# One denoising step of a hybrid trunk: the RWKV-7 stage divided along the tokens, and adaLN by single columns with stationary weights

## The chip, the cores and the metric

The kernel runs on one core of a Trainium2 chip. The metric is the device time of one execution, in microseconds (us). It was timed in several runs of the same program, and one further execution was profiled. The engines work side by side, each with its own queue, and wait for each other by semaphores: PE (TensorE, matrix products; PEld is its weight load), DVE (VectorE), ACT (ScalarE), POOL (GpSimd) and SP (SyncE, which here issues most transfers).

## The reference

One step of a two-layer network over a prompt of 256 tokens and a sample of 1024 tokens, 1024 channels. The even layer runs differential attention and a bidirectional RWKV-7 side by side; the odd layer mixes by Fourier transforms; each layer ends in a gated MLP. The change touches the RWKV and the modulation (adaLN). Cut to these:

```python
for l in range(DEPTH):                       # adaLN: 6144 columns of two conditions, for each layer
    mod = jax.nn.silu(c) @ w_ada[l] + b_ada[l]
...
def wkv_scan(state0, r, w, k, v, kk, a):     # 8 heads of 64, each direction by itself
    def step(S, inp):
        r_t, w_t, k_t, v_t, kk_t, a_t = inp
        sa = jnp.einsum("bhij,bhj->bhi", S, -kk_t)
        S = (S * w_t[:, :, None, :] + sa[..., None] * (kk_t * a_t)[:, :, None, :]
             + v_t[..., None] * k_t[:, :, None, :])
        return S, jnp.einsum("bhij,bhj->bhi", S, r_t)
...
for d in range(2):                           # forward and backward
    decay = jnp.exp(-jnp.exp(-jax.nn.softplus(-(w0 + jnp.tanh(wd) @ w2)) - 0.5))
    a = jax.nn.sigmoid(a0 + ad @ a2)
    kd = k * (1 + (a - 1) * kvec[1])
    S, y = wkv_scan(s0[:, d], r, decay, kd, v, kk, a)
    ys = ys + y
    bonus = bonus + jnp.sum(rh * kdh * r_k, axis=-1, keepdims=True) * vh
y = (layernorm_by_head(ys) * lnx[0] + lnx[1] + bonus) * (sigmoid(gd) @ g2)
```

## The kernel before

The heads are taken as 4 pairs (128 channels each). Time is cut into chunks of 64 tokens (C = 64). Inside a chunk the recurrence is a triangular system, so that a chunk's work is a handful of small matrix products, and only a 64 x 64 state for each head and direction goes from chunk to chunk. A *unit* is one direction of one pair over 256 tokens (4 chunks).

The stage has five *jobs*, one after the other: the sample of each pair (16 chunks, both directions, 8 units), and at last the prompt of all four pairs (8 units). The steps of a job, with the lines of the page:

- `job_prep`, 16 steps: `piece_prep` loads r, k, v of 256 tokens, sums squares by head (`hs_ps`, L737) and transposes v (`fl_ps`, L747). `unit_values` makes decays and the scaled k, r (`lora_ps` L753, scan L810, `bk` L838 to L844, `bkw` L847, `bd` L854). `unit_products` makes the products inside the chunks (`G_ps` L866), masks them (DVE, L870), gathers the diagonal 32 x 32 blocks (`il`, L873), sums the bonus and transposes `bkw`.
- `inverses`: a forward substitution of all 32 x 32 blocks of the job at once, on DVE alone: two transposes (L918, L919), 31 pairs of a product (L928) and a sum (L932), each on the result of the one before, two transposes back (L938, L939). Behind it stand the *corrections* of the units: T is copied into `tz` (ACT, L961), products mq (L965), ms (L969), gv (L975), tb (L983) and their copies on ACT (L987, L988).
- `chains`, 16 steps: at each, for both directions, state times keys (`ch`, L1035), `sav` from it (DVE, L1044), the state's increment (L1054), the new state (`sbd`, DVE, L1069, one instruction for each head), and the output (`y_ps`, L1080, L1082). The last output sum is DVE's L1092.
- `job_post`: y is normalised by head, gains and bonus are added, the gate is multiplied in (L1111 to L1143).

The modulation's columns that later stages need (20 blocks of 512 columns) are made beside this, by `ada_blocks`. A block loads weights in pieces of 256 KB (`ada_w`), multiplies them as the moving operand (128x512, L188) with the two conditions as stationary ones, copies the result (L195), and turns it into columns by four 128x2 products (L199).

All engines run in program order. `run` sets it: it takes steps of several generators in turns, in the proportion of the numbers beside them. So a job's chains (13 steps) stand beside 11 steps of the next job's preparation and 29 steps of adaLN; the last 3 chain steps stand beside the inverse, 5 steps of preparation beside the corrections. The preparation of job 0 is written ahead of all that, and the scheduler places it between the last tiles of the attention (`attn_tiles`, whose last instruction for each tile is `yt`, L568). Tiles with the same tag share buffers; G tiles have 6 slots for each direction.

Of the kernel before, what the change touches and what calls it, by code (L numbers as in the profile page):

```python
# [2 lines left out]

# [34 lines left out]
def host_tables():  # L38
# [36 lines left out]
    # columns: cos of channel frequencies 0 .. 64, sin of 1 .. 63 (and its negative)  # L75
# [23 lines left out]
def hybrid_step(ctx: ExitStack, tc: tile.TileContext, i: dict, o: dict):  # L99
# [16 lines left out]
    yab_d = tc.dram_tile([D, T], F32, name="yab_d")  # L116

    def reverse_rows(dst, src, a, n):
# [20 lines left out]
    def mm3(ps, a, b, first, last):  # L139
        """ps += a.T @ b for operands split into (hi, lo) float32r parts."""  # L140
# [5 lines left out]
    # modulation by channel [part, cond, block]; its gates (parts 2, 5) also by row, in mod_d  # L146
# [27 lines left out]
    def ada_steps(l, j, wp, pp, tag, nb, kn, wb, sb):  # L174
        """Columns 512 j of the modulation, in steps; its weights come by kn blocks."""
# [47 lines left out]

    def mod_cols(l, part):
        """[128, cond, KD] columns of one part of the modulation."""
# [4 lines left out]
    def hcols(pair, q, t0, n):  # L230
        """Tokens t0 .. t0 + n of part q (hi, lo) of one channel block; its tiles are (sample, prompt) by part."""
# [49 lines left out]
    def norm_scale(pl, tj, f, xs):  # L281
        """xs = f * rms(f) ** -1 of [128 tokens, D]; tj: (tag, bufs) of the squares."""
# [7 lines left out]
    def norm_tile(pl, tt, pp, tag, nb, xs, t0, hh, A, B):  # L290
        """Modulated, channel-major parts hh[k] = (hi, lo) of the 128 scaled tokens xs from t0."""
# [26 lines left out]
    def post_norm(xp, f, gg, res_ap, out_ap, rows=128, skip=0):  # L318
        """out = res + gate * rmsnorm(f); f [rows, D] in SBUF, overwritten."""
# [12 lines left out]
    # ================= layer 0: mixer input =================  # L332
    with ExitStack() as st:
# [44 lines left out]
        # values  # L378
# [33 lines left out]
        # queries, keys and RWKV projections, with the differential attention beside them  # L412
        with ExitStack() as st2:
# [35 lines left out]
            def do_fb(ti):  # L449
# [18 lines left out]
                if ti in (12, 14):  # L468
                    # wd: tanh; gd: sigmoid = 0.5 tanh(x / 2) + 0.5
# [16 lines left out]
            # -(exp(s0) - exp(s1) + lam_init)  # L486
# [27 lines left out]
                    # exp(s - max of the chunk) and its sum, by chunks of the keys  # L514
# [14 lines left out]
                    # factors exp(max of the chunk - max) / sum, times -lambda for the second map  # L529
# [107 lines left out]
    def out_weights(fw, wp, ks):  # L637
        """Rows of the even layer's output projection, split."""
# [9 lines left out]
    def out_product(fw, fo, po, t0):  # L648
        """The even layer's output projection of 128 tokens."""
# [15 lines left out]
    # ================= layer 0: RWKV-7 =================  # L665
    with ExitStack() as st:
        # by the times at which the memory becomes free and is needed again: lt from the chains on, eg from the
        # preparation on; ex (units that the last job does without), ep and li (preparation and inverses) are given
        # back before the last chains
# [5 lines left out]
        li = pool(st_d, "li", side="right")  # L675
        pp = pool(st, "pp2", space=PSUM)
        st_0 = ExitStack()
        PG = [pool(st_0, "p0", space=PSUM, side="right")]
# [14 lines left out]
        nc.vector.tensor_scalar(out=wa0, in0=wa0, scalar1=0.5, scalar2=None, op0=ALU.mult)  # L693
        kv1h = eg.tile([128, 2, 4], F32, name="kv1h")
        nc.vector.tensor_scalar(out=kv1h[:, 0, :], in0=kv[:, 1, :], scalar1=0.5, scalar2=None, op0=ALU.mult)
        nc.vector.tensor_scalar(
            out=kv1h[:, 1, :], in0=kv[:, 1, :], scalar1=-0.5, scalar2=1.0, op0=ALU.mult, op1=ALU.add
        )
        bonk = eg.tile([128, 4, 2], F32, name="bonk")
        for p in range(4):  # L700
            nc.vector.tensor_scalar(out=bonk[:, p, :], in0=bones, scalar1=kv[:, 2, p:p + 1], scalar2=None, op0=ALU.mult)
        cmask = eg.tile([128, 256], F32, name="cmask")
# [3 lines left out]
        sbd = [[lt.tile([128, 128], F32, name=f"sbd{d}{j}") for j in range(4)] for d in range(2)]  # L706
        for d in range(2):
            for j in range(4):
                nc.gpsimd.memset(sbd[d][j], 0.0)
        # b and k by head; T, by direction: the rest stays zero  # L710
        bds = [ep.tile([128, 4, 2, 128], F32, name=f"bd{j}") for j in range(2)]
        tzs = [[li.tile([128, 4, 2, 64], F32, name=f"tz{d}{j}") for j in range(2)] for d in range(2)]
        for t_ in bds + tzs[0] + tzs[1]:
            nc.gpsimd.memset(t_, 0.0)
        nw = [0, 0, [0, 0]]
        slot = [0, 0]
        LOB = 1
        NA = 13
        NB = 5
        A0, A1, A2, B1, B2, B3, B4 = 0, 16, 8, 29, 0, 0, 0  # L720
        NT, NCJ = 8, 16
        NP, NTP, NCP = 256, 2, 4
# [3 lines left out]
        jobs = [[(p, NP * j) for j in range(4)] for p in range(4)]  # L726
        jobs.append([(p, LS) for p in range(4)])

        c3 = lambda t: t.rearrange("p (c s) -> p c s", s=C)

        fl = lambda t: t.rearrange("p a b -> p (a b)")

        def head_sums(src, wt, out, acc):
            """out[tok, tile, head] (+)= sum over channels of src [channel, tok] wt [channel, head]."""
            ps = PG[0].tile([128, NTP, 2], F32, tag="g", bufs=2, name="hs_ps")
            for j in range(NTP):
                nc.tensor.matmul(ps[:, j, :], lhsT=src[:, j * 128:(j + 1) * 128], rhs=wt, start=True, stop=True)  # L737
            if acc is None:
                nc.vector.tensor_copy(out, ps)
            else:  # L740
                nc.vector.tensor_tensor(out=out, in0=ps, in1=acc, op=ALU.add)

        def flips(n, src):
            """Transposes of n 128 x 128 blocks src(j) into one bank."""
            ps = PG[0].tile([128, 4, 128], F32, tag="g", bufs=2, name="fl_ps")
# [4 lines left out]
        def lora(first, p, d, src, w, which, out):  # L750
            """out = tanh(0.5 (w0 + src @ w)) for the pair's channels."""
            ps = PG[-1].tile([128, NP], F32, tag="g" if first else "lo", bufs=2 if first else LOB, name="lora_ps")
            nc.tensor.matmul(ps, lhsT=w[HS[d], which, :], rhs=src[HS[d], which, :], start=True, stop=True)  # L753
            nc.scalar.activation(out, ps, AF.Tanh, bias=wa0[:, which, d, p:p + 1], scale=0.5)

        def piece_prep(J, j):
            p, t0 = J["pcs"][j]
            j0 = NTP * j
            if J.get("wp") != p:
                J["wp"] = p  # L760
                J["w"] = ep.tile([128, 2, 128], F32, tag="w2", bufs=2, name="w2")
                for e, nm in enumerate(("rwkv_w2", "rwkv_a2")):
                    for d in range(2):
                        nc.sync.dma_start(out=J["w"][HS[d], e, :], in_=i[nm][0, d, :, p * 128:(p + 1) * 128])
            r = ep.tile([128, NP], F32, tag="r", bufs=4, name="r")
            k = ep.tile([128, NP], F32, tag="k", bufs=4, name="k")
            v = ep.tile([128, NP], F32, tag="tmp", bufs=2, name="v")
            nc.sync.dma_start(out=k, in_=fb_d[4 + p, :, t0:t0 + NP])
            nc.sync.dma_start(out=v, in_=fb_d[8 + p, :, t0:t0 + NP])
            nc.sync.dma_start(out=r, in_=fb_d[p, :, t0:t0 + NP])  # L770
            # kk = k kv0 / sqrt(sum over the head + 1e-12); kkh = 0.5 kk
# [3 lines left out]
            head_sums(sq, bones, ss, None)  # L775
            nc.scalar.copy(J["vt"][:, j0:j0 + NTP, :], flips(NTP, lambda e: v[:, e * 128:(e + 1) * 128]))
# [6 lines left out]
            kkh = ep.tile([128, NP], F32, tag="kkh", bufs=4, name="kkh")  # L783
# [1114 lines left out]
```

## Time and profile before

| what | us |
|---|---|
| median of 3 runs | 3827.24 |
| lowest, highest run | 3824.96, 3835.42 |
| span of the profiled execution | 3829.1 |
| busy in the span: PE, DVE, ACT, POOL | 3568.9, 1984.3, 1381.8, 570.5 |
| first inverse's start, last output sum's start | 725.3, 1609.6 |
| chains, first to last `sav` (five jobs) | 852.8 to 1603.2 |
| corrections, first to last tb | 803.2 to 1560.7 |

The profile gives no other time for its execution than the span, which is 1.9 us above the median. A busy PE is not PE at its peak: the clock that was granted to it is a column of its own in the tables by window, and 0.50 there means that a product takes twice as long. A group's busy time is a sum over the instructions of one line, and can overlap itself, since products are pipelined; the distance from start to start is the better price where PE never waits.

### The profile page before, as it was taken

The numbers are of one execution on the slowest core, as the hardware profiler recorded it, in microseconds if no ns is written. First come the engines' busy times: TensorE is split into PE (matmuls) and PEld (weight loads), VectorE is DVE, ScalarE is ACT, GpSimd is POOL, SyncE is SP. The second block draws the span as 40 slices with busy tenths as digits, with TensorE's granted clock in tenths as the row PEclk, the third lists the DMA queues.
The fourth block names the chain that finished last, engine by engine and source line by source line (L and its number), as shares of the span: only waits on it lengthen the run. The fifth ranks groups of instructions, "written<-read, shape, count | busy, mean of one in ns | idle before, by whom it ended". The sixth has DMA issues, their size and how long they took to land.

```text
span 3829.1 us, 53177 instructions
## 1 busy us (share of the span) xinstructions
PE 3568.9 (93%) x20712; PEld 2865.0 (75%) x20712; DVE 1984.3 (52%) x4009; ACT 1381.8 (36%) x2892; POOL 570.5 (15%) x937
## 2 busy tenths in 40 slices
PE   6999999898999786999999999998968999999997
PEld 5888887554646575788888888887757888888886
DVE  4276677837372847565344434446554344443446
ACT  4266566652535353463212111113443211121211
POOL 3111112411212222053000000004141000000003
PEclk8999999879897967999999999999988999999999
DMA  6232323223342210455111111104341111111113
GB/s 215 92 97 81 98 67 86 83 76 118 97 119 75 67 29 7 125 151 140 39 33 45 39 34 39 39 31 172 126 115 32 39 39 34 44 34 39 39 31 129
DMA packets 293469, 286.60 MB, mean 75 GB/s; under 512 B 52955, under 2 KB 229051, under 8 KB 293217
## 3 DMA queue, kind: packets, MB, share of 16 engines
q1 hardware_dynamic: 228864, 223.09, 18.9%
q0 software_dynamic: 15952, 40.46, 3.1%
q10 hardware_dynamic: 48400, 19.65, 2.1%
q8 instruction: 163, 2.67, 0.3%
q14 instruction: 90, 0.73, 0.1%
HBM read 233.65 MB, written 51.51 MB: 74 GB/s over the span
## 4 chain that ended last, share of the span: by engine, by line
PE 79%; DVE 7%; DMA 4%; ACT 3%; issue 2%; POOL 1%; ACTq 0%; DVEq 0%; SPq 0%; POOLq 0%
PE a_ps L142 11%; PE a_ps L143 10%; PE a_ps L141 10%; PE b_ps L142 5%; PE b_ps L141 5%; PE b_ps L143 5%; PE ada_ps L188 3%; PE tb_ps L983 2%; PE f_ps L141 2%; PE f_ps L142 2%; PE f_ps L143 2%; PE sc_ps L520 2%; PE G_ps L866 2%; PE pv_ps L556 2%; DMA ada_w<-in_w_ada 1%
## 5 line engine op out<-in xcount | busy, mean ns | idle before, releaser
L141 PE MATMUL a_ps<-hh,f_hi 128*128 128x512 f32 (+1 forms) x2144 | 761.4, 356 | 18.7 <-ACT f_hi L136 14.5
L142 PE MATMUL a_ps<-hl,f_hi 128*128 128x512 f32 (+1 forms) x2144 | 762.5, 356 | 3.1 <-POOL hl L308 3.1
L143 PE MATMUL a_ps<-hh,f_lo 128*128 128x512 f32 (+1 forms) x2144 | 761.1, 355 | 0.2 <-DVE f_lo L137 0.2
L1313 DVE TENSOR_TENSOR acc<-b_ps,acc 128x512 f32<-128x512 f32 x400 | 270.4, 689 | 405.7 <-PE b_ps L143 405.6
L141 PEld LDWEIGHTS a_ps<-hh,f_hi 128*128 128x128 f32 x2144 | 404.6, 189 | 83.6 <-ACT f_hi L136 15.0
L142 PEld LDWEIGHTS a_ps<-hl,f_hi 128*128 128x128 f32 x2144 | 404.7, 189 | 68.3 <-POOL hl L308 4.8
L143 PEld LDWEIGHTS a_ps<-hh,f_lo 128*128 128x128 f32 x2144 | 405.0, 189 | 63.0 <-DVE f_lo L137 0.9
L142 PE MATMUL b_ps<-d_lo,mh 128*128 128x512 f32 x880 | 348.4, 396 | 0.0
L143 PE MATMUL b_ps<-d_hi,ml 128*128 128x512 f32 x880 | 346.8, 394 | 0.0
L141 PE MATMUL b_ps<-d_hi,mh 128*128 128x512 f32 x880 | 341.5, 396 | 3.6 <-DVE acc L1313 3.1
L137 DVE TENSOR_TENSOR f_lo<-f_raw,f_hi 128x512 fp32r<-128x512 f32 x176 | 114.5, 691 | 307.2 <-ACT f_hi L136 305.0
L1259 POOL MEMSET gp<- 128x1 f32 x44 | 4.3, 98 | 1572.7 <-DVE cv L1278 1572.7
L136 ACT CAST d_hi<-d_raw 128x512 fp32r<-128x512 f32 x88 | 54.5, 621 | 488.4 <-PE b_ps L143 474.6
L141 PE MATMUL f_ps<-hh,w_hi 128*128 128x512 f32 (+1 forms) x552 | 198.5, 360 | 0.5 <-ACT nk L444 0.5
L141 PEld LDWEIGHTS b_ps<-d_hi,mh 128*128 128x128 f32 x880 | 165.3, 188 | 45.0 <-DVE acc L1313 4.5
L188 PE MATMUL ada_ps<-ada_w,csil 128*32 128x512 f32 x384 | 172.6, 721 | 28.0 <-DMA ada_w<-in_w_ada 26.4
L142 PE MATMUL f_ps<-hl,w_hi 128*128 128x512 f32 (+1 forms) x552 | 197.3, 357 | 0.0
L143 PE MATMUL f_ps<-hh,w_lo 128*128 128x512 f32 (+1 forms) x552 | 197.3, 357 | 0.0
L143 PEld LDWEIGHTS b_ps<-d_hi,ml 128*128 128x128 f32 x880 | 164.9, 187 | 40.7
L142 PEld LDWEIGHTS b_ps<-d_lo,mh 128*128 128x128 f32 x880 | 165.1, 188 | 37.3
L1270 ACT COPY gp<-a_ps 128x512 f32<-128x512 f32 (+1 forms) x134 | 68.1, 508 | 341.9 <-PE a_ps L143 341.9
L1290 DVE TENSOR_TENSOR md<-a_ps,cv 128x512 f32<-128x512 f32 (+1 forms) x134 | 79.5, 595 | 163.8 <-PE a_ps L143 100.5
(564 smaller groups left out, 6768.1 us busy)
## 6 DMA issues: line engine op xcount, KB each, us to landing
f_raw<-in_w_ffn_in SPq DMA_DIRECT2D x176, 256.0 KB, 3.2
ada_w<-in_w_ada SPq DMA_DIRECT2D x160, 256.0 KB, 2.8
d_raw<-in_w_ffn_out SPq DMA_DIRECT2D x88, 256.0 KB, 2.9
nx<-x_d SPq DMA_DIRECT2D x24, 512.0 KB, 4.9
w_raw<-in_w_in_even SPq DMA_DIRECT2D x23, 512.0 KB, 4.2
lo_in<-fb_d SPq DMA_DIRECT2D x40, 256.0 KB, 2.8
rx<-x_d SPq DMA_DIRECT2D x20, 512.0 KB, 5.1
ada_w<-in_w_ada SPq DMA_DIRECT2D x16, 512.0 KB, 6.8
```

What stands on the lines that cost most here:

```text
L137: nc.vector.tensor_tensor(out=lo, in0=src, in1=hi, op=ALU.subtract)
L141: nc.tensor.matmul(ps, lhsT=a[0], rhs=b[0], start=first, stop=False)
L142: nc.tensor.matmul(ps, lhsT=a[0], rhs=b[1], start=False, stop=False)
L143: nc.tensor.matmul(ps, lhsT=a[1], rhs=b[0], start=False, stop=last)
L188: nc.tensor.matmul(ps[32 * q:32 * q + 32], lhsT=csil[:, k0 + k, :], rhs=w[:, k, :], start=(k0 < 4), stop=(k0 >= 4),)
L520: nc.tensor.matmul(ps[:, :nn], lhsT=qs[:, m, a, :], rhs=ks[m][:, n0:n0 + nn], start=(a == 0), stop=(a == 1),)
L556: nc.tensor.matmul(pv, lhsT=wt[:, kb, :], rhs=vt[:, kb, :], start=(kb == 0), stop=(kb == nk // 128 - 1))
L866: nc.tensor.matmul(pss[h][:, c, :], lhsT=bd[:, c, h, :], rhs=kr[:, c].rearrange("p a s -> p (a s)"), start=True, stop=True,)
L983: nc.tensor.matmul(ps[:, e, h, :], lhsT=tz[:, c + e, h, :], rhs=g[:, c + e, h, 64:192], start=True, stop=True,)
L1270: nc.scalar.copy(gp[:, o0:o0 + n], up(ws, t0, n))
L1290: nc.vector.tensor_tensor(out=md, in0=ps, in1=cv[:, o0:o0 + n], op=ALU.mult)
L1313: nc.vector.tensor_tensor(out=acc[j][:, cs], in0=ps, in1=acc[j][:, cs], op=ALU.add)
```

## The change

**Rounds for jobs.** The stage is divided along the tokens: five rounds, each with 4 chunks (256 tokens) of all four pairs and both directions. In round q the forward direction takes tokens from 256 q, the backward one from 256 (3 - q); round 4 is the prompt. A round has two *half rounds* of two pairs (4 units). Three half rounds have buffers at once (G, kr: slot n % 3). A round has one inverse for its 8 units; corrections and chains go by half rounds.

**Chains.** A chain step takes two pairs and two directions together: four states in flight, 4 steps for each half round. The unknowns are added in place, into G's own rows, by one DVE instruction over both pairs; before it was one for each direction. The state updates remain one for each head, pair and direction.

**v by token.** v's transposes go to memory (`vtok_d`) and are loaded for each unit in the corrections (`sv`) and for each post; k's normed form is kept in memory between the two directions' rounds (`kkh_d`), and y too (`y_d`), since the two directions reach a token in different rounds. Posts are made for 256 tokens of all pairs, beside the inverses of rounds 3 and 4, and at the end.

**Engines.** The first factor of `kr`, th + 1, wcol and the tz copies go to POOL; POOL also copies `sv` into G. The two multiplications of `bk` become one.

**adaLN.** The remaining 80 columns of 128 are made one by one: the weights (128 x 128, loaded as 512 KB a column) are the stationary operand, the two conditions the moving one, 8 matmuls of 128x2 each, and an ACT activation adds the bias. 20 columns go with each of the rounds 0 to 3. Their PSUM tile is one of the two "g" buffers that lora, G, head sums and transposes use as well; before, adaLN and lora had buffers of their own from job 1 on.

The diff, cut to its core:

```diff
+    def ada_columns(parts, wp, wb, ps_tile):
+        for l, part in parts:
+            m = modc[l][:, part]
+            for k1 in range(KD):
+                c0 = part * D + k1 * 128
+                w = wp.tile([128, KD, 128], F32, tag="ada_c", bufs=wb, name="ada_c")
+                nc.sync.dma_start(
+                    out=w, in_=i["w_ada"][l, :, c0:c0 + 128].rearrange("(k p) c -> p k c", p=128)
+                )
+                ps = ps_tile()
+                for k in range(KD):
+                    nc.tensor.matmul(ps, lhsT=w[:, k, :], rhs=csil[:, k, 0:2], start=(k == 0), stop=(k == KD - 1))
+                nc.scalar.activation(
+                    m[:, :, k1], ps, AF.Identity, bias=bcol[:, l, part * KD + k1:part * KD + k1 + 1]
+                )
...
+            sl = n % 3
+            H["G"] = gk.tile([128, 2, 2, NCP, 2, 192], F32, tag=f"G{sl}", name="G")
...
-                nc.scalar.copy(tv[bs, :, bs], src[ls, :, n0:n0 + nn_].rearrange("s t n -> s n t"))
+                sv = lt.tile([128, NCP, 128], F32, tag="sv", bufs=2, name="sv")[64:128]
+                nc.sync.dma_start(
+                    out=sv, in_=vtok_d[t0:t0 + NP, p * 128:(p + 1) * 128].rearrange("(c s) n -> s c n", s=C)
+                )
+                    nc.gpsimd.tensor_copy(tv[bs, :, bs], src[ls, :, n0:n0 + nn_].rearrange("s t n -> s n t"))
...
+                for d in range(2):
+                    gu = G[0:64, d, :, cl[d], :, 0:64]
+                    if not zero:
+                        u = cps[d][0:64, 0:256].rearrange("p (a h s) -> p a h s", a=2, h=2)
+                        nc.vector.tensor_tensor(out=gu, in0=u, in1=gu, op=ALU.add)
...
-        run((inv, 9), (ada, A1))
-        run((inv, 9), (prep, NB), (ada, A2))
-        for jn in range(5):
-            run((chain, NA), (prep, 16 - NB), (ada, B1))
-            run((chain, 16 - NA), (inv, 9), (ada, B2))
-            run((post, 5), (inv, 9), (prep, NB), (ada, B3))
+        A1, A2, A3, A4, A5 = 5, 2, 3, 2, 8
+        run((begin(0), 9))
+        run((begin(1), 9))
+        for q in range(5):
+            inv = inverses(R[q])
+            pa_ = begin(2 * q + 2)
+            run((inv, 9), (pa_, 4), (ada, A1), (ps_, 16))
+            co = [corrections(R[q], H[2 * q + e]) for e in range(2)]
+            ch = [chains(H[2 * q + e]) for e in range(2)]
+            run((inv, 9), (co[0], 4), (pa_, 1), (ada, A2))
+            y_tiles(q)
+            run((ch[0], 5), (co[1], 4), (pa_, 4), (ada, A3))
+            pb_ = begin(2 * q + 3)
+            run((ch[1], 5), (pb_, 2), (ada, A4))
+            run((pb_, 9), (ada, A5))
```

Here `begin(n)` gives the preparation of half round n, `ps_` the posts, `co` the corrections, `ch` the chains.

**How the order moves.** First place: PE at the end of the attention (sc, wt, pv, ya are the attention's products; hs or kk, fl, lora the first preparation's). Before:

```order
L520 MATMUL sc_ps<-ks,qs 128x256 x4
L737 MATMUL hs_ps<-bones,sq 128x2 x2
L747 MATMUL fl_ps<-ident,v 128x128 x2
L520 MATMUL sc_ps<-ks,qs 128x512 x2
L556 MATMUL pv_ps<-av,wt 128x128 x6
L520 MATMUL sc_ps<-ks,qs 128x512 x4
L747 MATMUL fl_ps<-ident,rsx 128x128 x2
L753 MATMUL lora_ps<-lo_in,w_7310 128x256
```

After:

```order
L586 MATMUL wt_ps<-ident,e 128x128 x2
L590 MATMUL pv_ps<-avp,wt 128x128 x2
L600 MATMUL ya_ps<-ident,ya 128x128
L775 MATMUL kk_ps<-bones,sq 128x2 x2
L782 MATMUL fl_ps<-ident,v 128x128 x2
L782 MATMUL fl_ps<-ident,rsx 128x128 x2
L789 MATMUL lora_ps<-lo_in,w_7311 128x256 x2
```

The last product of the attention now stands ahead of the first of the preparation. The preparation's small tables (`mk`, `bones`, `kv`) lie where tiles of the attention were.

Second place: PE beside an inverse, from the last products of the chains (before) or of the preparation (after) to the first mq, which needs the inverse. Before, beside the third inverse:

```order
L1080 MATMUL y_ps<-sbd_7280,kr 64x128
L1082 MATMUL y_ps<-sav,G 64x64 x4
L188 MATMUL ada_ps<-ada_w,csil 32x512 x2
L975 MATMUL gv_ps<-sav,G 64x64 x8
L199 MATMUL ada_ps_12499<-sel,ada_mp 128x2 x4
L188 MATMUL ada_ps<-ada_w,csil 32x512 x8
L199 MATMUL ada_ps_12695<-sel,ada_mp 128x2 x4
L188 MATMUL ada_ps<-ada_w,csil 32x512 x2
L965 MATMUL mq_ps<-tz_7295,G 32x32 x8
```

After, round 1:

```order
L782 MATMUL fl_ps<-ident,bkw 128x128 x4
L239 MATMUL ada_ps<-csil,ada_c 128x2 x32
L789 MATMUL lora_ps<-lo_in,w_9753 128x256 x2
L239 MATMUL ada_ps<-csil,ada_c 128x2 x8
L789 MATMUL lora_ps<-lo_in,w_9753 128x256 x2
L239 MATMUL ada_ps<-csil,ada_c 128x2 x8
L926 MATMUL G_ps<-kr,bd_7297 128x128 x8
L775 MATMUL bon_ps<-bonk,ta 128x2 x2
L782 MATMUL fl_ps<-ident,bkw 128x128 x4
L239 MATMUL ada_ps<-csil,ada_c 128x2 x8
L789 MATMUL lora_ps<-lo_in,w_9753 128x256 x2
L239 MATMUL ada_ps<-csil,ada_c 128x2 x16
```

Nine columns (72 matmuls), the values of three units and the products of one now stand beside the inverse; before it was adaLN alone, and the end of the chains.

Third place: PE in the corrections. Before, they stand with the next preparation and adaLN:

```order
L969 MATMUL ms_ps<-mqs,xn 32x32 x8
L975 MATMUL gv_ps<-sav,G 64x64 x8
L866 MATMUL G_ps<-kr,bd_7292 128x128 x8
L983 MATMUL tb_ps<-G,tz_7296 64x128 x4
L188 MATMUL ada_ps<-ada_w,csil 32x512
L983 MATMUL tb_ps<-G,tz_7296 64x128 x4
```

After, those of the second half round stand between the chain steps of the first:

```order
L1082 MATMUL ch<-sbd_7281,kr 64x128 x2
L1036 MATMUL tb_ps<-G,tz_7299 64x128 x8
L1082 MATMUL ch<-sbd_7283,kr 64x128 x2
L789 MATMUL lora_ps<-lo_in,w_12279 128x256
L239 MATMUL ada_ps<-csil,ada_c 128x2 x2
L1091 MATMUL ch<-G 64x64 x4
L1115 MATMUL y_ps<-G 64x64 x2
L1018 MATMUL mq_ps<-tz_7298,G 32x32 x8
L1023 MATMUL gv_ps<-sv,G 64x64 x8
```

A chain's products (`ch`, `y_ps`) now wait in the same queue behind corrections of the other half.

More of the change, by code (lines that the diff above doesn't have):

```diff
@@ L2 @@
 from contextlib import ExitStack
+from itertools import chain
 import numpy as np
@@ L715, in hybrid_step @@
[L715 to L727, printed above, removed]
+        bon = eg.tile([128, T // 128, 4, 2], F32, name="bon")
+        sbd = [[[lt.tile([128, 2, 128], F32, name=f"sbd{hf}{d}{v}") for v in range(2)] for d in range(2)] for hf in range(2)]
@@ L748, in flips, with lora @@
             return ps[:, 0:n, :]
[L750 to L766, printed above, removed]
+        def lora(H, pp_, d, which, out):
+            p = 2 * H["hf"] + pp_
+            ps = ps_g([128, NP], "lora_ps")
+            nc.tensor.matmul(
+                ps, lhsT=H["w"][HS[d], which, pp_ * 128:pp_ * 128 + 128], rhs=H["src"][HS[d], which, :],
+                start=True, stop=True,
+            )
+            nc.scalar.activation(out, ps, AF.Tanh, bias=wa0[:, which, d, p:p + 1], scale=-0.5 if which else 0.5)
@@ L974, in inverses @@
                         for h in range(2):
                             nc.tensor.matmul(
-                                pv[:, c, h, :], lhsT=g[64:128, c, h, 0:64], rhs=sav[64:128, NCP * je + c, HS[h]],
+                                ps[:, e, h, :], lhsT=tz[:, c + e, h, :], rhs=g[:, c + e, h, 64:192],
                                 start=True, stop=True,
                             )
-                    for c in range(0, NCP, 2):
-                        ps = pp.tile([64, 2, 2, 128], F32, tag="y", bufs=2, name="tb_ps")
+                    nc.scalar.copy(g[0:64, c:c + 2, :, 64:192], ps)
@@ new lines, in corrections, with initial_states @@
+                yield
+        ver = [[0, 0], [0, 0]]
+        yt = {}
+        def initial_states(hf):
+            for d in range(2):
+                S = sbd[hf][d][0]
+                for pp_ in range(2):
+                    p = 2 * hf + pp_
+                    si = lt.tile([64, 2, 64], F32, tag="mqs", bufs=2, name="si")
+                    nc.sync.dma_start(out=si, in_=i["state_wkv"][0, 0, d, 2 * p:2 * p + 2].rearrange("h i j -> i h j"))
+                    ps = pp.tile([128, 64], F32, tag="t", bufs=2, name="si_ps")
+                    nc.tensor.transpose(ps, si.rearrange("i h j -> i (h j)"), ident[0:64, 0:64])
+                    for h in HS:
+                        nc.scalar.copy(S[h, pp_, h], ps[h])
@@ new lines, in y_tiles, with chains @@
+        def y_tiles(q):
+            for d in range(1 if q == 4 else 2):
+                t = yt[q, d] = lt.tile([128, NTP, 4, 128], F32, tag="y", bufs=2, name="y")
+                if q in (2, 3):
+                    t0 = first_token(q, d)
+                    nc.sync.dma_start(
+                        out=t.rearrange("p a b s -> p a (b s)"),
+                        in_=y_d[t0:t0 + NP].rearrange("(a p) c -> p a c", p=128),
+                    )
+        def chains(H):
+            q, hf = H["q"], H["hf"]
+            G, KR, W = H["G"], H["kr"], H["wc"]
+            yps = [pp.tile([128, 2, NTP, 128], F32, tag=f"y{d}", name="y_ps") for d in range(2)]
+            for j in range(NCP):
+                cl = (j, NCP - 1 - j)
+                zero = q == 4 and j == 0
+                last = q == 3 and j == NCP - 1
+                S = [sbd[hf][d][ver[hf][d]] for d in range(2)]
+                cps = [pp.tile([128, 512], F32, tag=f"c{d}", name="ch") for d in range(2)]
+                for d in range(2):
+                    u = cps[d][0:64, 0:256].rearrange("p (a b) -> p a b", a=2)
+                    if not zero:
+                        for e in range(2):
+                            nc.tensor.matmul(u[:, e, :], lhsT=KR[:, d, e, cl[d], 0, :], rhs=S[d][:, e, :], start=True, stop=True)
+                for d in range(2):
+                    gu = G[0:64, d, :, cl[d], :, 0:64]
+                    if not zero:
+                        u = cps[d][0:64, 0:256].rearrange("p (a h s) -> p a h s", a=2, h=2)
+                        nc.vector.tensor_tensor(out=gu, in0=u, in1=gu, op=ALU.add)
+                    if not last:
@@ new lines, in chains @@
+                for d in range(2):
+                    c = cl[d]
+                    for e in range(2):
+                        y = yps[d][HS[c % 2], e, c // 2, :]
+                        for h in range(2):
+                            nc.tensor.matmul(
+                                y[:, HS[h]], lhsT=G[:, d, e, c, h, 64:128], rhs=G[:, d, e, c, h, 0:64],
+                                start=(h == 0), stop=(zero and h == 1),
+                            )
+                        if not zero:
+                            nc.tensor.matmul(y, lhsT=KR[:, d, e, c, 1, :], rhs=S[d][:, e, :], start=False, stop=True)
@@ new lines, in chains @@
+                yield
+            for d in range(2):
+                if q == 4:
+                    yo = yt[4, 0]
+                else:
+                    yo = yt[q, d]
+                yo = yo[:, :, 2 * hf:2 * hf + 2, :].rearrange("p a b s -> p b a s")
+                if q < 2 or (q == 4 and d == 0):
+                    nc.scalar.copy(yo, yps[d])
+                else:
+                    nc.vector.tensor_tensor(out=yo, in0=yps[d], in1=yo, op=ALU.add)
+                if q < 2 and hf == 1:
+                    t0 = first_token(q, d)
+                    nc.sync.dma_start(
+                        out=y_d[t0:t0 + NP].rearrange("(a p) c -> p a c", p=128),
+                        in_=yt[q, d].rearrange("p a b s -> p a (b s)"),
+                    )
```

547 lines of the change are left out of this document (259 added, 288 removed).

## The prediction

> **What bounds the kernel now.** I read the page's totals first, then the windows by stage, then the passes and groups of the RWKV stage, then single rows. The totals name TensorE:
>
> ```profile
> PE 3568.9 (93%) x20712; PEld 2865.0 (75%) x20712; DVE 1984.3 (52%) x4009; ACT 1381.8 (36%) x2892; POOL 570.5 (15%) x937
> ```
>
> That average hides the stages. The windows below have: stretch, length, busy time of PE, PEld, DVE, ACT, POOL (instructions), granted clock, DMA share, GB/s.
>
> ```profile
> 609.00:735.00 126.00, 106.03 (x640) 84.67 (x638) 108.99 (x310) 109.10 (x293) 47.97 (x72) 0.92 0.26 70
> 852.00:936.00 84.00, 82.29 (x669) 50.59 (x667) 49.38 (x160) 24.50 (x46) 11.79 (x16) 1.00 0.38 114
> 1153.00:1245.00 92.00, 85.41 (x641) 59.89 (x638) 23.72 (x60) 48.26 (x97) 19.48 (x22) 0.77 0.25 74
> 1321.00:1345.00 24.00, 3.00 (x33) 2.70 (x32) 22.18 (x51) 3.18 (x5) 0.00 (x0) 0.51 0.00 1
> 1485.00:1509.00 24.00, 3.02 (x33) 2.70 (x32) 22.23 (x51) 3.15 (x5) 0.00 (x0) 0.51 0.00 0
> 1509.00:1556.00 47.00, 43.15 (x470) 37.86 (x471) 10.77 (x29) 28.32 (x56) 5.51 (x3) 0.74 0.13 42
> 1556.00:1609.00 53.00, 46.25 (x450) 36.94 (x449) 35.48 (x105) 19.92 (x43) 0.00 (x0) 0.94 0.38 114
> 1609.00:3829.00 2220.00, 2128.77 (x10564) 1769.02 (x10562) 1029.41 (x1581) 579.13 (x1063) 246.38 (x449) 0.98 0.21 65
> ...
> 811.00:840.00 29.00, 28.69 (x185) 18.53 (x186) 2.26 (x5) 13.17 (x27) 2.44 (x3) 0.50 0.16 50
> ```
>
> 609 to 735 is the end of the attention with the first preparation beside it: ACT and DVE are as full as PE. 852 to 936 is a job's chains with the next preparation and adaLN beside them: PE is full at full clock. 1153 to 1245 are the corrections: PE looks busy, but at a clock of 0.77. 1321 and 1485 are ends of inverses: DVE works alone, PE does 3 us of 24. 1509 to 1556 and 1556 to 1609 are the last corrections and the prompt's chains. The last row but one, 2220 us, is code that the diff leaves alone. 811 to 840 is a first half of corrections: busy 28.69 of 29 us, at half clock.
>
> So the stage has two losses: TensorE has nothing to do in the inverses, and runs slowly after them. Its frame is in first and last starts:
>
> ```profile
> L568 DVE TENSOR_SCALAR yt<-ya_ps,subln x13: 292/346/352, 604.7 to 737.7; 128x128 f32<-128x128 f32 x13
> L918 DVE STREAM_TRANSPOSE nn<-il x5: 1937/1968/1976, 725.3 to 1463.1; 64x1024 f32<-64x1024 f32 x5
> L866 PE MATMUL G_ps<-kr,bd x640: 270/275/583, 648.5 to 1465.2; 128*128 128x128 f32 x160
> L1092 DVE TENSOR_TENSOR y<-y_ps,y x10: 681/691/693, 936.3 to 1609.6; 128x512 f32<-128x512 f32 x10
> ```
>
> The first inverse starts at 725.3, the last y is added at 1609.6: 884.3 us for five jobs. The whole sum is made on this frame.
>
> **The start (first preparation).** In the changed order all attention tiles stand ahead of the first `kk_ps` on PE; before, `hs_ps` came between them. The small tables are loaded later, and two half rounds (8 units, as many as job 0 had) are prepared with nothing beside them. Attention alone must end earlier than 737.7, since it loses its company. A unit's ACT copies are two of each of these:
>
> ```profile
> L873 ACT COPY il<-G 32x256 f32<-32x256 f32 x80 | 50.5, 632 | 18.8 <-DVE G L870 17.9
> L854 ACT COPY bd<-bk 64x512 f32<-64x512 f32 x80 | 49.2, 615 | 18.2 <-DVE bk L844 17.2
> ```
>
> That is 2.5 us, with its tanh, exps and the transposed copy about 5 (an estimate), so 40 us for 8 units. Lower bound: ACT was the limit and gives all 40 us back, so attention ends at 698, and the preparation needs ACT's 40 again plus a few us of latency: 742. Upper bound: attention ends at 737.7 as before and the preparation takes some 60 us: 798. The preparation alone lies between 40 and the 76.8 us from 648.5 to 725.3 that it took in company; I take 63, since each unit is a chain over five engines with two PSUM buffers. Attention I let end at 712, between the bounds. First inverse: 775, that is 50 us late.
>
> **A round's TensorE work.** Starts in stretches where PE never waits give the price of a pass (a float32 matmul is two):
>
> ```profile
> 875.28 2.05 PE L866 MATMUL G_ps<-kr,bd 128*128 128x128 f32 x16
> 877.26 0.43 PE L1035 MATMUL ch<-sbd,kr 128*64 128x128 f32 x2
> ...
> 1170.21 1.96 PE L983 MATMUL tb_ps<-G,tz 128*64 128x128 f32 x16
> 1172.10 0.62 PE L188 MATMUL ada_ps<-ada_w,csil 128*32 128x512 f32 x1
> ...
> 1173.08 0.69 PE L965 MATMUL mq_ps<-tz,G 32*32 32x32 f32 x16
> 1173.69 1.14 PE L975 MATMUL gv_ps<-sav,G 64*64 64x64 f32 x16
> 1174.76 0.43 PE L983 MATMUL tb_ps<-G,tz 128*64 128x128 f32 x2
> ...
> 1034.96 1.05 PE L199 MATMUL ada_ps<-sel,ada_mp 128*128 128x2 f32 x8
> 1035.95 0.70 PE L753 MATMUL lora_ps<-lo_in,w 64*128 64x256 f32 x2
> 1036.58 0.62 PE L188 MATMUL ada_ps<-ada_w,csil 128*32 128x512 f32 x2
> ```
>
> G: 1.98/16 = 0.124 us; tb 0.118; mq 0.038; gv 0.067; lora 0.315; a 128x2 matmul on 128 stationary columns 0.124. The units are the same as before: G, tb, gv, mq have 128 passes a round each, lora 31, together 15.9 + 15.1 + 8.6 + 4.9 + 9.8 = 54 us for 543 passes, 0.100 on average. The other 465 passes (ms, the chains' four products, transposes, head sums) I take at the same mean, as the chain passes have 64 columns on one side: 46 us. A round of 8 units needs 100 us at full clock.
>
> **adaLN.** Before, 80 columns cost 320 passes of 128x512 and 160 of 128x2:
>
> ```profile
> 868.05 1.05 PE L188 MATMUL ada_ps<-ada_w,csil 128*32 128x512 f32 x2
> 869.02 0.34 PE L1054 MATMUL ch<-sav,G 128*64 128x64 f32 x4
> ...
> L188 PE MATMUL ada_ps<-ada_w,csil 128*32 128x512 f32 x320 | 160.5, 702 | 27.7 <-DMA ada_w<-in_w_ada 26.1 <-DVE mod L202 0.8 <-ACT ada_row L216 0.3
> ```
>
> 0.97/2 x 320 + 160 x 0.124 = 175 us. Now a column is 8 matmuls, 16 passes of the L199 kind: 1.98 us, 80 of them 158. That saves 17 us of TensorE at full clock. Each column adds an ACT activation of 128x2 and takes one of the two PSUM buffers that G, lora and the transposes share; I cost both at nothing, ACT being at 24.50 of 84 us beside the chains; if that cover goes, a buffer held for one column delays a G by its 2 us. The 27.7 us that L188 idled, mostly on its weights, I don't count as won: 80 loads of 512 KB replace 160 of 256 KB in the same two buffers, and on SP's queue the stores of v and k by token now wait ahead of them. A round carries 20 columns: 40 us. Its sum is 140.
>
> **The phases of a round.** First the inverse. It is the same 62 dependent DVE operations over all 8 units' chunks, so there are five of them as before:
>
> ```profile
> L928 DVE TENSOR_TENSOR tm<-nn,x 128x31 f32<-128x31 f32 (+15 forms) x155 | 54.6, 352 | 3.6
> L932 DVE TENSOR_TENSOR x<-x,tm 128x31 f32<-128x31 f32 (+15 forms) x155 | 58.7, 378 | 3.6
> L870 DVE TENSOR_TENSOR G<-G_ps,mk 128x512 f32<-128x512 f32 x80 | 54.8, 686 | 31.4 <-PE G_ps L866 30.4
> ...
> 1505.57 1.25 DVE L938 STREAM_TRANSPOSE xt<-x 128x1024 f32<-128x1024 f32 x1
> 1506.74 1.89 DVE L939 STREAM_TRANSPOSE xn<-x 128x1024 f32<-128x1024 f32 x1
> ```
>
> (54.6 + 58.7)/5 + 3 us of gaps + four transposes (6.4 us) = 32 us. Before, the last three chain steps ran beside it; now three units' values and one unit's G products do, and the remaining columns of the round before. Their DVE work (two masks of 0.686 us, scans and products, some 3.5 us a unit) stretches it to 45. TensorE has 9 columns (17.8 us), three units' loras (3.7) and one G set (3.5) in that time: 25 us at full clock, 50 at half, so it is covered either way only just. What is left of the round, 140 - 25 = 115 us, runs in the corrections, in the four-chain steps beside corrections, and in the preparation. If that is as dense as 852 to 936 (669 passes in 84 us, 0.126 against 0.100 to 0.124 unmixed), it takes 117. A round: 45 + 117 = 162 us.
>
> DVE in the chains falls: one 64x2x2x64 addition where two of 64x128 stood. I cost that at nothing, DVE having 49.38 of 84 us there; the eight state updates of a step remain. The copies that POOL gets (tz, sv, kr) are hidden while POOL has 11.79 us of work in 84; if it falls behind, mq waits for tz.
>
> **Posts and the last round.** y is normalised only in rounds 3 and 4, beside the inverse, on the same DVE:
>
> ```profile
> 1610.28 1.22 DVE L1111 TENSOR_REDUCE ln_m<-y 128x16 f32<-128x1024 f32 x1
> 1611.75 1.23 DVE L1113 TENSOR_TENSOR y<-y,ln_m 128x1024 f32<-128x1024 f32 x1
> ```
>
> A post has some eight such passes, 9.5 us, and two fall into each: +19 us in round 3, +19 in round 4. Last round: inverse 32 + 19 + 1; half the corrections, 47/2 = 23.5; four chain steps beside the other half, 30; four steps alone, 24 (DVE has twice the 35.48/16 = 2.2 us of a step of before, plus latency); y 2: 132 us.
>
> **Sum.** 775 + 4 x 162 + 19 + 132 = 1574, against 1609.6: 36 us less. The profiled span is 3829.1 us, 2 above the median of 3827.24; so 3793 on the span and 3792 on the median. With rounds of 171 us nothing would be gained: the margin is 9 us a round. A measurement of this kernel tells about 0.3%, 11.5 us, from no change.
>
> **Rivals.**
> *The inverse hides (faster).* If columns and early preparation fill TensorE wholly during the inverse at full clock, a round is its sum, about 143: 4 x 19 less, 3716. Against it: 25 us of work is all that stands there, and PE's clock was 0.51 beside each inverse. 0.08.
>
> *Half rounds in series (no change).* There are three G slots; the second half's preparation needs the slot of the half whose chains run in the same round. If it then starts only behind the other half's chains, a round is 45 + 30 + 47 (corrections; chains with corrections, by their PE sums) + 18 (four steps) + 32 (four units at 63/8) = 172: 3832 on the span, 3830. For it: the next inverse needs all eight units' blocks. Against: the first units of that half are written between the chain steps. 0.16.
>
> *The clock stays low (slower).* Before, only the corrections ran cold (0.77, 0.74), and even 811 to 840, with PE busy throughout, stayed at 0.50. Now corrections lie beside the chains that used to be at 1.00, and a half-filled inverse precedes them in every round. At 0.77 the first half's corrections take 35 for 27 us, the mixed phase 61 for 47: a round of 184. 4 x 22 more: 3880. It decides from 171 on. 0.25; and 0.12 that the start (798) and slow units alone bring it there, 3845 or so.
>
> [...]
>
> [...]
>
> **Chances and range.** Forecast (rounds of 150 to 167) 0.39, hidden inverse 0.08: faster 0.47. Same 0.16. Slower 0.25 + 0.12 = 0.37. The forecast's own range is 3740 to 3815; the range for 8 in 10 runs from the hidden inverse, 3712, to the cold rounds, 3885.
>
> **What would show it.** The first inverse near 775, with attention's last yt near 712; five inverses 160 to 165 us apart, each about 45 us; the clock at 1.00 where chains and corrections mix; 128x2 passes at 0.124 us. Wrong, if inverse starts lie over 171 apart, if the clock is near 0.75 between them, if PE waits for ada_c, or if the first inverse starts before 742 or after 798.

## The result, and the profile after

The changed kernel takes 3954.68 us (median of 4 runs, 3952.93 to 3960.63) where the kernel before took 3826.1 beside it: a ratio of 1.0338, interval 1.0313 to 1.0362. It is 129 us slower; the forecast was 35 us faster, and the time lies 70 us above the range.

The totals of the page say that TensorE has become busier, and every other engine but POOL less busy:

```profile
PE 3702.0 (94%) x21512; PEld 3137.2 (79%) x21512; DVE 1945.5 (49%) x3685; ACT 1351.6 (34%) x2867; POOL 713.2 (18%) x1180
```

The frame of the stage, by first and last starts (attention's `yt`, the inverses, the last output sum, out products behind the stage):

```profile
L602 DVE TENSOR_SCALAR yt<-ya_ps,subln x16: 332/346/352, 559.8 to 696.7; 128x128 f32<-128x128 f32 x16
L968 DVE STREAM_TRANSPOSE nn<-il x5: 1917/1930/1954, 790.3 to 1580.0; 64x1024 f32<-64x1024 f32 x5
L1131 DVE TENSOR_TENSOR y<-y_ps,y x10: 683/691/693, 1303.8 to 1720.6; 128x512 f32<-128x512 f32 x10
L144 PE MATMUL o_ps<-o_hi,oyh x160: 387/389/632, 1721.4 to 1841.6; 128*128 128x512 f32 x160
```

The first inverse is 65.0 us later than before. From there to the last output sum it is 930.3 us, 46.0 more than the 884.3 before. The first product of the MLP started at 1714.2 before and starts at 1842.3, so the way to it from the last output sum has grown from 104.6 to 121.7 us, by 17.1. Together 128.1 us. What lies behind it is 5 us shorter in this pair of profiles.

The windows show how the rounds look inside (same columns as in the prediction):

```profile
697.00:790.30 93.30, 69.07 (x286) 53.26 (x285) 42.10 (x91) 50.66 (x109) 54.90 (x87) 0.59 0.28 81
790.30:1580.00 789.70, 739.86 (x5781) 660.99 (x5782) 374.05 (x870) 293.21 (x606) 268.69 (x382) 0.71 0.30 86
1580.00:1718.60 138.60, 103.79 (x991) 90.09 (x991) 73.97 (x180) 41.98 (x92) 30.82 (x33) 0.71 0.22 71
...
833.60:840.60 7.00, 7.00 (x34) 6.94 (x34) 4.46 (x5) 2.97 (x6) 5.59 (x9) 0.50 0.27 77
800.00:850.00 50.00, 41.50 (x203) 36.76 (x203) 35.70 (x76) 18.30 (x39) 22.38 (x32) 0.50 0.31 91
900.00:950.00 50.00, 49.22 (x577) 43.66 (x575) 24.94 (x75) 19.25 (x40) 13.10 (x19) 0.96 0.23 71
850.00:900.00 50.00, 49.55 (x423) 43.77 (x421) 10.41 (x29) 18.28 (x38) 14.48 (x23) 0.67 0.18 53
```

The four jobs before are this row:

```profile
725.30:1463.10 737.80, 655.20 (x4968) 429.40 (x4969) 408.24 (x1117) 332.49 (x659) 166.82 (x210) 0.85 0.27 83
```

Over four rounds TensorE is busy for 740 of 790 us, and its mean clock is 0.71; in the four jobs it was 0.85. 800 to 850 is an inverse, with the columns beside it, and the first corrections behind it, at half clock. 850 to 900 are corrections: full, at 0.67. Groups of the page's kind tell what that costs; the first has the passes of the columns, the second those of G, which are the same work as before, and the third is G in the kernel before:

```profile
L239 PE MATMUL ada_ps<-csil,ada_c 128*128 128x2 f32 x1280 | 223.3, 303 | 3.5 <-DMA ada_c<-in_w_ada 2.4 <-ACT sq_ps L1186 1.1
L926 PE MATMUL G_ps<-kr,bd 128*128 128x128 f32 x640 | 139.8, 395 | 5.0 <-ACT bd L913 1.9 <-ACT mod L240 1.6 <-ACT G L943 1.5
L866 PE MATMUL G_ps<-kr,bd 128*128 128x128 f32 x640 | 97.7, 301 | 3.0 <-ACT bd L854 0.9 <-POOL bkw L847 0.8 <-DVE kr L831 0.6
```

A G pass is at 395 ns on average where it was 301 before; the 640 of them are 42 us busier (97.7 before). A group's busy time was called a sum above, which it is not: 640 passes of 395 ns would be 253 us, not 139.8, so time in which passes overlap counts once. Single rows show a column set at both clocks:

```profile
833.64 6.99 PE L239 MATMUL ada_ps<-csil,ada_c 128*128 128x2 f32 x32
840.56 1.06 PE L1018 MATMUL mq_ps<-tz,G 32*32 32x32 f32 x16
...
957.80 1.95 PE L239 MATMUL ada_ps<-csil,ada_c 128*128 128x2 f32 x16
959.60 0.59 PE L775 MATMUL kk_ps<-bones,sq 128*128 128x2 f32 x4
```

At 957.80, at a clock of 1.00, the set of 16 passes takes 1.80 us to the next start, 0.113 a pass, somewhat under the price I had used. At 833.64 two sets take 6.92, 0.216 a pass: TensorE works without a break for 7 us (833.60 to 840.60 above, 7.00 of 7.00 us busy) and stays at half clock (0.50).

### The profile page after: what moved, and what is told of

Same layout as the page of the kernel before. It is cut to its first block, busy times and chain, and to the rows that moved or that the text cites. A ratio compares the mean times of both kernels' runs of the same rounds, so it can differ in the third digit from the quotient of the medians.

```text
span 3952.2 us, 54932 instructions
## 1 busy us (share of the span) xinstructions
PE 3702.0 (94%) x21512; PEld 3137.2 (79%) x21512; DVE 1945.5 (49%) x3685; ACT 1351.6 (34%) x2867; POOL 713.2 (18%) x1180
## 4 chain that ended last, share of the span: by engine, by line
PE 82%; DVE 5%; DMA 3%; ACT 2%; POOL 2%; issue 2%; ACTq 0%; DVEq 0%; SPq 0%; POOLq 0%
PE a_ps L145 10%; PE a_ps L146 10%; PE a_ps L144 10%; PE b_ps L145 5%; PE b_ps L144 5%; PE b_ps L146 5%; PE ada_ps L239 4%; PE G_ps L926 3%; PE tb_ps L1036 3%; PE f_ps L144 2%; PE f_ps L146 2%; PE f_ps L145 2%; PE pv_ps L590 2%; PE sc_ps L554 2%; PE lora_ps L789 2%
## 5 line engine op out<-in xcount | busy, mean ns | idle before, releaser
L239 PEld LDWEIGHTS ada_ps<-csil,ada_c 128*128 128x128 f32 x1280 | 218.9, 264 | 22.7 <-ACT th L793 8.5
L239 PE MATMUL ada_ps<-csil,ada_c 128*128 128x2 f32 x1280 | 223.3, 303 | 3.5 <-DMA ada_c<-in_w_ada 2.4
```

The source lines that it names most:

```text
L239: nc.tensor.matmul(ps, lhsT=w[:, k, :], rhs=csil[:, k, 0:2], start=(k == 0), stop=(k == KD - 1))
```

## The experiments

The theory formed on these rows, called A: the clock follows how many columns TensorE moves, not how long it is busy. A 128x2 pass loads 128 columns of weights (a load of 128x128, 264 ns of mean duration in L239's group) and moves two; a stretch of them counts as idle (0.50 from 833.60 to 840.60; 0.51 from 1321 to 1345 before, where TensorE was busy for 3.00 of 24 us), and takes the work behind it down (0.67 from 850 to 900). The rival, B: TensorE is cold because it waits, in the inverses and in a preparation with nothing beside it (0.59 from 697.00 to 790.30). All times are medians; the ratio is to the kernel before on the same chip. That kernel took 3823 to 3833 us beside the experiments, so a difference of under 10 us between two of them tells nothing. The code is shortened to what changes.

**1. Sixty-four times the columns.** Every column product moves the conditions' 32 columns four times over:

```diff
-  nc.tensor.matmul(ps, lhsT=w[:, k, :], rhs=csil[:, k, 0:2], ...)
+  nc.tensor.matmul(ps, lhsT=w[:, k, :], rhs=csil[:, k, :].unsqueeze(1).to_broadcast([128, 4, 32]), ...)
```

> The changed kernel, with each adaLN column product moving 128 columns (the two conditions' 32 columns read four times) where it moved 2; only the first two results are used, so the output is the same. Theory A (the clock follows moving columns: a stretch of 128x2 passes, 0.21 us each at half clock and about 9 moving columns a us, counts as idle): although TensorE has 64 times the columns to stream, the clock rises in the preparation and corrections, and the time falls to 3830 to 3900 us. Theory B (the clock is low because TensorE waits in the inverses and in the bare preparation, whatever the columns are): no gain, 3945 to 3975 us, since a 128x128 pass costs the 0.124 us of a 128x2 pass at full clock.

3841.31 us, ratio 1.0032 [1.0016, 1.0048]: 113 us faster than the change, with the loads, order and buffers of the change. The groups and windows of this kernel, in the same places as above:

```profile
L239 PE MATMUL ada_ps<-csil,ada_c 128*128 128x128 f32 x1280 | 189.7, 309 | 14.0 <-DMA ada_c<-in_w_ada 12.5 <-DVE bon L938 0.3 <-ACT e L876 0.2
L926 PE MATMUL G_ps<-kr,bd 128*128 128x128 f32 x640 | 96.4, 305 | 7.6 <-ACT bd L913 5.2 <-ACT G L943 2.0 <-issue 0.3
```

```profile
787.20:1459.30 672.10, 607.49 (x5792) 532.36 (x5793) 376.72 (x871) 293.00 (x607) 269.52 (x382) 0.92 0.35 101
...
800.00:850.00 50.00, 40.23 (x283) 35.92 (x282) 36.49 (x77) 21.93 (x45) 24.86 (x35) 0.76 0.37 103
850.00:900.00 50.00, 49.68 (x601) 44.38 (x602) 17.68 (x52) 21.54 (x45) 15.27 (x25) 1.00 0.18 52
```

The same 1280 passes take 190 us in place of 223, though each moves 128 columns; G is back at 305 ns, near the 301 of before; the corrections from 850 to 900 run at 1.00 with 601 passes where 423 were. Four rounds take 672.1 us where they took 789.7. B has no place for that.

**2. How many columns.** The same edit with 32 and with 64 columns.

> The changed kernel with 32 moving columns in each adaLN column product (the conditions' own 32, of which two are used), between the 2 of the change and the 128 that gave 3841 us. [...] If any more columns help in proportion: 3900 to 3930 us. If it was something else in the wide form (a longer product, other buffers): about 3850 us.

> The changed kernel with 64 moving columns in each adaLN column product; 2 gave 3955 us, 32 gave 3940, 128 gave 3841. [...] If the gain goes in proportion to the columns: 3895 to 3915 us.

3939.81 us (1.0302 [1.0279, 1.0325]) and 3897.17 us (1.0166 [1.0147, 1.0186]). With 2, 32, 64 and 128 columns: 3955, 3940, 3897, 3841. For a gain in proportion to the columns I had expected 3900 to 3930 at 32 and 3895 to 3915 at 64; for a clock that needs more columns than that, which was my estimate and is shown by no run, 3930 to 3965 and 3925 to 3950. At 32 the second held and the first missed, at 64 it was the other way round. The gain grows with the columns, slowly up to 32; the mean clock of the four rounds goes with it, 0.71, 0.74, 0.79 and 0.92. Where the clock switches, and whether the rows that a product uses count as well, is not settled by these runs.

**3. The other way round.** The weights moving (128x256 passes, conditions stationary), at the places of the columns. The rounds are kept; the loads come in pieces of 256 KB again, and DVE adds the bias:

```diff
-  for k in range(KD):
-      nc.tensor.matmul(ps, lhsT=w[:, k, :], rhs=csil[:, k, 0:2], ...)
+  for k in range(KD):                                   # ps [128, 256]
+      nc.tensor.matmul(ps[32 * (k % 4):32 * (k % 4) + 32], lhsT=csil[:, k, :], rhs=w[:, k, :], ...)
+  nc.scalar.copy(mp, ps)
+  for e in range(2):
+      nc.tensor.matmul(ps2[:, e, :], lhsT=mp[:, e, :], rhs=sel, ...)
```

> The changed kernel with adaLN the old way round: weights as the moving operand, 128x256 passes with the conditions stationary, then 128x2 products that turn the row into columns; loads, PSUM buffers and places in the order stay those of the columns. Theory A: TensorE has 640 passes of 256 columns (about 155 us at full clock) and 160 of 128x2 instead of 1280 of 128x2: the clock rises, 3840 to 3900 us. Theory B: about the changed kernel's 3955, 3940 to 3980 us.

3829.14 us, 1.0007 [0.9989, 1.0025]: the whole loss is gone, and a little more than A's range allowed. The window of its four rounds warns against reading the mean clock as time:

```profile
789.10:1453.80 664.70, 581.78 (x5331) 456.95 (x5331) 379.57 (x928) 285.84 (x568) 267.89 (x382) 0.79 0.33 102
```

Its clock is 0.79 against 0.92 with the wide columns, and its rounds are 7 us shorter. TensorE has less to do here (581.78 us busy against 607.49) and is idle for longer (82.92 us against 64.61), and the mean counts these stretches too. What a low clock costs in them this run doesn't show.

**4. The columns alone.** The kernel before, its five jobs kept, with the columns in place of the blocks, two and then 128 columns wide (adaLN's share of the turns is scaled to its fewer steps):

```diff
-  ada = ada_blocks([(0, j) for j in range(4, 12)] + [(1, j) for j in range(12)], li, PG[1], "ada", 1, 1, 2, 1)
+  ada = ada_columns([(0, 2), ..., (1, 5)], li, 2, lambda s=[128, 2]: PG[1].tile(s, F32, tag="ada", bufs=1, name="ada_ps"))
```

> The kernel before, with nothing changed but adaLN: the 80 single columns with stationary weights in place of the 20 blocks of 512, in the adaLN buffer of its own, at the same share of each stage. Theory A: the columns cool the chains, which were at a clock of 1.00: 3860 to 3930 us. Theory B: 17 us of TensorE less, 3805 to 3830 us.

> The kernel before with the single columns as in the experiment that gave 3976 us, but 128 moving columns in each product. If the 148 us that the columns cost there came from the clock, they go: 3810 to 3840 us, what TensorE saves (17 us by my price of a column) being the most it can gain on 3826. If part of the cost was the columns' loads or their buffer, 3860 to 3930 us remain.

3975.89 us (1.0411 [1.037, 1.0452]) and 3789.17 us (0.9882 [0.9856, 0.9909]). So the second half of the change, by itself, costs more (about 147 us) than the whole change did. And by moving 128 columns it gains 44 us instead, more than the 17 that I had as a limit. Four jobs with narrow and with wide columns:

```profile
727.80:1602.10 874.30, 831.01 (x5765) 718.19 (x5766) 403.58 (x1090) 341.39 (x718) 164.48 (x209) 0.64 0.24 69
```

```profile
726.80:1416.60 689.80, 620.82 (x5764) 526.98 (x5765) 405.32 (x1089) 340.58 (x718) 167.74 (x209) 0.91 0.30 88
```

737.8 us before at 0.85, 874.3 at 0.64, 689.8 at 0.91: the blocks had not kept TensorE fully warm either. That the whole surplus over 17 us comes from the clock is an inference; no run separates it from the loads.

**5. The rounds without adaLN, and the jobs without it.**

> The changed kernel without the 80 adaLN columns of this stage (their place is filled with constants, so the results downstream are wrong); it shows the rounds alone. Theory A: what goes is 223 us of busy TensorE and the cold clock that they spread: 3710 to 3780 us, with the clock in the mixed phases at 1.00. Theory B: the inverses and the preparation leave TensorE idle and cold anyway, so 3790 to 3850 us.

> The kernel before without the adaLN blocks of this stage (constants in their place, so the results downstream are wrong), as the counterpart of the changed kernel without its columns (3779 us). If the rounds by themselves are worth what they lose at the start and the end, this lies at 3770 to 3790 us. If the rounds are a loss of their own (the start 60 us later), 3690 to 3750 us. If they are a gain, over 3795 us.

3779.04 us (0.9885 [0.986, 0.991]) and 3737.6 us (0.9775 [0.9743, 0.9806]). The first lies at the upper end of A's range, just under B's; it doesn't tell them apart. Together they tell what the rounds are worth: 41 us lost. The inverses' starts, first the rounds, then the jobs:

```profile
L968 DVE STREAM_TRANSPOSE nn<-il x5: 1934/1955/1960, 796.0 to 1401.7; 64x1024 f32<-64x1024 f32 x5
```

```profile
L918 DVE STREAM_TRANSPOSE nn<-il x5: 1944/1949/1961, 728.7 to 1373.6; 64x1024 f32<-64x1024 f32 x5
```

The start is 67.3 us later; four rounds take 605.7 us where four jobs take 644.9, 39.2 less. The rounds do gain; the start takes more, and the end keeps some. The windows of these stretches, rounds first, show that theory B has a part too:

```profile
796.00:1401.70 605.70, 490.51 (x4560) 413.18 (x4560) 377.36 (x864) 271.64 (x526) 267.98 (x378) 0.79 0.16 46
728.70:1373.60 644.90, 517.47 (x4476) 419.48 (x4477) 401.46 (x1082) 318.16 (x633) 166.17 (x204) 0.76 0.10 30
```

Without any adaLN the mean clock is 0.79 and 0.76. The narrow columns take it from there to 0.71 and 0.64, the dense ones to 0.92 and 0.91.

**6. The start.** In the wide-column kernel, the memory of the small tables and of the first two G slots is moved away from the attention's tiles:

```diff
   lt = pool(st, "lt")
+  gz = pool(st, "gz")
   eg = pool(st, "eg")
...
-  gk = ex if sl == 1 else eg
+  gk = (eg, ex, gz)[sl]
```

> The changed kernel with 128 moving columns in the adaLN products (3841 us), and one G slot that is used late placed at the low end of the memory, so that the small tables and the first two slots lie where the attention has no tiles: the first preparation then stands between the attention's last tiles again. If the late start (first inverse at 790 where it was 725) is a cost by itself, the first inverse moves to 735 to 755 and the time to 3790 to 3810 us. If attention and preparation only compete for ACT and DVE, 3830 to 3845 us.

3800.29 us, 0.9933 [0.9911, 0.9955]: some 40 us faster than without (41 by the medians, 38 by the ratios), from the place of a few tiles. The first inverse starts 37 us earlier, at 750.1 for 787.2:

```profile
L969 DVE STREAM_TRANSPOSE nn<-il x5: 1947/1958/1982, 750.1 to 1416.2; 64x1024 f32<-64x1024 f32 x5
```

With the moving blocks of experiment 3 in place of the wide columns:

> The rounds with adaLN in moving blocks of 256 columns (3829 us) and the first preparation beside the attention again, as in the kernel that went from 3841 to 3800 us. If the two gains add: 3780 to 3800 us, the fastest of all. If the dense columns were what made the early start pay, 3800 to 3825 us.

3789.70 us, 0.9896 [0.9869, 0.9922]: the gains add, 39 us on 3829. It and the jobs with wide columns are the fastest kernels here that do all the work, equal within their intervals.

**7. Idle products for warmth.** The kernel before, with 100 products of 128x256 that nothing uses, while DVE ends the inverse:

```diff
+  wps = pp.tile([128, 256], F32, tag="ch1", name="warm_ps")
+  for _ in range([12, 8, 40, 40, 0][J["jn"]]):
+      nc.tensor.matmul(wps, lhsT=S[0][0], rhs=csil.rearrange("p k c -> p (k c)"), start=True, stop=True)
```

> The kernel before with idle work added: behind the last chain step of the sample jobs TensorE multiplies 12, 8, 40 and 40 times a state by 256 columns (100 products of 128x256, about 49 us at full clock, used by nothing), while DVE ends the inverse. Theory A: the corrections behind it start at full clock instead of 0.74 to 0.86, and the kernel gets faster: 3770 to 3815 us. Theory B (the corrections are slow because they wait for copies, and the clock follows from that): no gain, 3825 to 3850 us, since the products stand where TensorE was idle.

3824.53 us, 1.0003 [0.9988, 1.0018]: nothing. The windows are an inverse's end and the corrections behind it, twice:

```profile
1320.00:1345.00 25.00, 21.35 (x136) 18.28 (x135) 21.95 (x51) 4.48 (x8) 0.00 (x0) 0.98 0.00 1
1345.00:1413.00 68.00, 62.86 (x583) 53.28 (x582) 26.27 (x60) 45.91 (x94) 22.25 (x24) 0.80 0.11 31
...
1480.00:1503.00 23.00, 19.03 (x105) 16.48 (x104) 21.60 (x51) 2.03 (x3) 0.00 (x0) 0.96 0.00 0
1503.00:1551.00 48.00, 43.74 (x484) 38.41 (x483) 11.53 (x30) 29.36 (x58) 5.51 (x3) 0.74 0.13 41
```

The clock in the inverse went from 0.51 to 0.98 and 0.96, and the windows of the corrections behind it are still at 0.80 and 0.74. Finer rows show that the warmth didn't reach the corrections. The last idle product ends at 1339.8; then TensorE waits three times for ACT's copies, and from 1345 to 1350 it is at half clock:

```profile
1339.70 1.14 PE L975 MATMUL gv_ps<-sav,G 64*64 64x64 f32 x16
1342.15 0.69 PE L965 MATMUL mq_ps<-tz,G 32*32 32x32 f32 x16 [1.31 <-ACT tz L961]
1344.45 1.11 PE L969 MATMUL ms_ps<-mqs,xn 32*32 32x32 f32 x16 [1.61 <-ACT mqs L966]
1347.52 1.05 PE L965 MATMUL mq_ps<-tz,G 32*32 32x32 f32 x16 [1.96 <-ACT tz L961]
...
1345.00:1350.00 5.00, 2.45 (x30) 2.18 (x29) 0.00 (x0) 4.39 (x8) 0.00 (x0) 0.50 0.00 0
```

So the run didn't give the corrections a warm start, and it can't tell what keeps them cold: these waits, as B says (3824.53 is half a us below its range), or products that move 32 or 64 columns, as A would have it. Theory A, for the columns, stands by experiments 1 and 4 (0.71 to 0.92 and 0.64 to 0.91 with the moved columns), with 3 in agreement (0.71 to 0.79); its extension to the corrections is not shown.

## Why the prediction was wrong, by its own steps

- **adaLN, the price of a column: the step that failed.** I priced a 128x2 pass at full clock, 0.124 us, from a single row of 8 passes amid dense work, and called the edit a saving of 17 us. At full clock the price was about right (0.113 at 957.80). But 1280 of them bring the clock down, for themselves and for what stands beside them: 0.216 a pass at 833.64, 395 ns for a G pass, 0.71 over four rounds, where experiment 1 has 305 ns and 0.92. Put in place of the blocks, alone, they cost the kernel before 147 us; moving two columns in place of 128 cost the change some 113. With dense columns the sum for the rounds comes out: 4 x 162 + 19 = 667 us forecast, 672.1 measured in experiment 1, against 789.7 in the change. Part of that is luck, since two misses cancel: a round has 1140 passes beside adaLN (4560 in four rounds of experiment 5) for the 1008 that I took, and TensorE gets more done beside the inverse, in experiment 1 27 to 44 us for the 25 of the sum.
- **The start.** 775 forecast, 790.3 measured, within its bounds. Attention ended earlier than I took (696.7 for 712), but the bare preparation took 93 us for 63, beyond even the 77 that it had needed in company: TensorE's clock was 0.59 there, and POOL, which had got more of the unit, was busy for 55 of 93 us. Experiment 6 gives the worth of an early start, about 40 us, and shows that the place of tiles in memory had held it up.
- **The inverse.** Nearly right: from its first transpose to the start of its last, plus 1.9 us, five of them took 46 to 52 us, for 45. The clock of 0.51 that I put beside each inverse was that of two of their ends in the kernel before (1321 to 1345, 1485 to 1509); two others had 0.65 (936 to 959) and 0.72 (1125 to 1153).
- **The posts and the last round.** The last round took 141 us for 132. Round 3, which carries posts, took 220 us where the other three took 199, 182 and 188; 19 were allotted.
- **The end.** I charged nothing behind the last output sum; it was 17 us. Before, the first out product started at 1589.4, 20 us ahead of the last sum; now it starts at 1721.4, behind it. In the trace it follows a load of its input that lands at 1720.8, and its weights still land until about 1719; which of these holds it, and why they come so late, was not tried.
- **The rivals.** "The clock stays low" came true, with a chance of 0.25, and beyond its size, but mostly for another reason than it gave: it let the corrections cool the chains (184 us a round, 3880); the columns did (197). In the wide kernel corrections and chains mix at 1.00 (864 to 911). In the rounds without adaLN the first corrections are cold, as it said (843 to 870 at 0.78, 1290.8 to 1318 at 0.67), but the mixed phases behind them are at 0.93 and 1.00 (870 to 917, 1318 to 1365). So half of what it named is there; the 113 us came from the columns.
- **The clock.** How long TensorE is busy doesn't tell it: busy 49.55 of 50 us at 0.67, 7.00 us without a pause at 0.50. Experiment 1 changed the moved columns alone and the clock followed, from 0.71 to 0.92. That the corrections would run at full clock, as the 162 us of a round take it, was my estimate: 850 to 900 is at 0.67 in the change, at 1.00 in experiment 1. I kept a rival for a low clock, but didn't ask what the new passes would do to it, though 811 to 840 (28.69 of 29 us busy at 0.50) had shown that busy isn't enough.

## What to carry to other kernels

Price a matmul by its time, but ask also how many columns it moves: a stage full of products that move two columns ran at a mean clock of 0.71 here, at 0.92 when they moved 128, in profiles that show TensorE nearly full both times (739.86 of 789.70 us and 607.49 of 672.10). Turning operands round so that the long side moves was worth 126 us here; moving useless columns up to 128 was worth 113 and 187, for a few changed lines. And where a stage is rewritten, see which memory its first tiles take: the place of some tables and buffers decided 40 us.

## What the runs showed of the hardware

Adding work made the kernel faster: 64 times the moved columns, 113 us less, and the passes themselves went from 303 to 309 ns of mean duration while the time in which any of them ran fell from 223 to 190 us (they overlap, so starts lie closer). TensorE was busy for 7.00 of 7.00 us with narrow products and stayed at half clock (0.50). In experiment 7 the warmth was soon lost: the clock is 0.98 from 1320 to 1345, the idle products end at 1339.8 us, and from 1345 to 1350, with 2.45 of 5 us busy, the clock is 0.50. And four rounds at a mean clock of 0.79 (experiment 3) took 664.7 us, those at 0.92 (experiment 1) 672.1.
